# Two transformer blocks on one NeuronCore: the modulation summed on VectorE unit by unit, and the first block's values for both query tiles at once

## The chip, the cores and the metric

The kernel runs on one core of one Trainium2 chip. The metric is the device time of one execution in microseconds; where several runs are given, it is their median. The engines are named as in the profile: PE (TensorE), PEld (its weight loads), DVE (VectorE), ACT (ScalarE), POOL (GpSimd) and SP (SyncE), which issues the DMAs. Each engine takes its instructions in order; semaphores join them.

## The reference, cut to what matters

Two transformer blocks follow each other, each of two layers, on 256 tokens of width 1024, all in float32. The first block has two streams, the tokens `x` and a context `ctx` of 256 rows, and a modulation from two condition vectors: six vectors of 1024 numbers for each stream and layer, from `silu(c)` and `silu(c_ctx)` times a matrix of 1024 x 6144.

```python
for l in range(DEPTH):                       # DEPTH = 2
    mod = silu_c @ w_ada[l] + b_ada[l]       # stream x
    mod_c = silu_cc @ w_ada[l] + b_ada[l]    # stream ctx
    sh1, sc1, gt1, sh2, sc2, gt2 = jnp.split(mod[:, None, :], 6, axis=-1)
    csh1, csc1, cgt1, csh2, csc2, cgt2 = jnp.split(mod_c, 6, axis=-1)
    h = modulate(rms_norm(x, norm1_g[l]), sh1, sc1)        # h * (1 + scale) + shift
    hc = modulate(rms_norm(xc, norm1_g[l]), csh1, csc1)
    # projections of h and hc; ya: windowed attention, yb: full attention, 8 heads of 64 each
    x = x + gt1 * merge_branches(ya, yb, ga, gb, w_proj_a[l], w_proj_b[l], w_out[l])
    h2 = modulate(rms_norm(x, norm2_g[l]), sh2, sc2)
    x = x + gt2 * swiglu(h2, w_ffn_gate[l], w_ffn_up[l], w_ffn_down[l])
    if not last:
        # the same for xc, with csh2, csc2, cgt1, cgt2
```

The gates come first (`gt1` in the w_out step, `gt2` in the down step), shifts and scales in the norms. In layer 1 the context only gives keys and values, so of its modulation no more than `csh1` and `csc1` is used. The second block (three branches, no modulation) is not touched by the change.

## The kernel before

**Products.** Activations lie transposed, features on partitions, 512 columns for both streams in layer 0 and 256 in layer 1. Each weight product is made in split float32: a weight tile is loaded as 1 MB of raw numbers (`wload` L182, `rawp`, two tiles, by SP's queue), `wsplit` (L189) makes its high part on ACT (L197) and its low part on DVE (L198) into four buffers, and `product` (L201) issues three matmuls for each of eight row blocks: high times high (L204), low times high (L205), high times low (L206), into one of three PSUM banks `acc`. The splits are issued at a raised priority, so that they stand earlier in the engines' order than they are written.

**Stages of the first block, layer 0** (times in the profile): keys, values and queries of the first attention up to 83 us; the first attention woven with the projections of the second (83 to 220); the second attention woven with the first branch's gates and merge (to 336); the second branch's gates and merge (to 383); the w_out step `narrow` (L773) with the second norm (to 429); the feed-forward part in three parts of gate, up and down products (to 825); layer 1's first norm inside the last `narrow` (to 848); then layer 1.

**Modulation.** `ada` (L334) makes it in units of 512 of the 6144 columns, twelve to a layer. A unit loads four pieces of 512 KB of `w_ada` (L345; tile `araw`, two buffers), and for each piece PE makes four matmuls of 256 columns (L349) with a stationary tile `silu_c` of 32 columns of which two are used, one per stream; the four go to four groups of 32 partitions of one bank `sm` that a DVE reduce adds up later. ACT copies the unit's rows (L353), PE transposes them (L356, four at 128 columns), DVE reduces (L358), adds the bias (L361) and makes gains and halved gates (L363 to L367). The generator yields after each piece, and `tick` (L387) takes one step of the first generator in `pending`. Ticks stand in the queries, the merge, `narrow` and the feed-forward loop. Units 2, 0, 3 and 1 of layer 0 are made ahead of everything, up to 60 us. Units 4 to 11 are put in `pending` at L446; all twelve of layer 1 are put there at L805, behind the w_out step, and whatever is left is drained before the last down step of layer 0 (L890), since that step's `norm1` needs layer 1's first units.

**Attention.** `gqa_steps` (L477) goes over pairs of heads and query tiles of 128. For each it issues scores (L498, a mask matmul L501), the row maximum on DVE (L502), and then the values of the query tile before: `values_of` (L542) transposes the two heads' probabilities (L551), ACT copies them to `pts` (L553, four buffers), and PE multiplies the values (`vt`, up to four key tiles) with them into bank `y` (L557): 64 value rows, 128 query columns a matmul. After the second query tile the result is split (L560, L561).

Of the kernel before, what the change touches and what calls it, by code (L numbers as in the profile page):

```python
# [9 lines left out]
F32 = mybir.dt.float32  # L10
# [4 lines left out]
ALU = mybir.AluOpType  # L15
AX = mybir.AxisListType

P = 128
D = 1024
KD = D // P  # L20
S = 256
# [54 lines left out]
def two_blocks(ctx: ExitStack, tc: tile.TileContext, A, out: bass.AP, tap=None):  # L76
    nc = tc.nc
# [245 lines left out]
    silu_c = cp.tile([P, KD, 32], F32, name="silu_c")  # L323
# [4 lines left out]
    V.tensor_scalar(out=silu_c[:, :, 0:2], in0=th.rearrange("p (s k) -> p k s", s=2), scalar1=0.5, scalar2=None, op0=ALU.mult)  # L328
# [3 lines left out]
    hgate = [cp.tile([P, 2, 8, 2], F32, name=f"hgate_{l}") for l in range(DEPTH)]  # L332

    def ada(l, units, tiles, banks=(sm_bank, sm_bank)):  # L334

        for u in units:
# [22 lines left out]
            tl = slice(4 * u, 4 * u + 4)  # L359
            M = mod[l][:, tl, :]  # L360
            V.tensor_add(out=M, in0=d, in1=colsb[:, 48 * l + 4 * u:48 * l + 4 * u + 4].unsqueeze(2).to_broadcast([P, 4, 2]))  # L361
            kind, ks = u // 2, slice(4 * (u % 2), 4 * (u % 2) + 4)
            if kind in (1, 4):  # L363
                gain, vec = (gain1, g_norm1) if kind == 1 else (gain2, g_norm2)
                V.scalar_tensor_tensor(out=gain[l][:, ks, :], in0=M, scalar=1.0, in1=vec[l][:, ks].unsqueeze(2).to_broadcast([P, 4, 2]), op0=ALU.add, op1=ALU.mult)
            elif kind in (2, 5):
                V.tensor_scalar(out=hgate[l][:, kind // 3, ks, :], in0=M, scalar1=0.5, scalar2=None, op0=ALU.mult)  # L367
            yield

    def early():  # L370
# [7 lines left out]
        for tag, bufs in (("g", 4), ("pts", 4), ("ks", 4), ("qst", 2), ("pr", 2)):  # L378
            for _ in range(bufs // 2):
                yield [ba.tile([P, 512], F32, name="early", tag=tag, bufs=bufs) for _ in range(2)]  # L380

    def araw():
        return b1.tile([P, 1024], F32, name="araw", tag="araw", bufs=2),

    pending = []

    def tick():  # L387

        if pending:
            if next(pending[0], 0) is not None:  # L390
                pending.pop(0)
                tick()

# [52 lines left out]
    pending.append(ada(0, range(4, 12), araw))  # L446
# [30 lines left out]
    def gqa_steps(heads):  # L477
# [6 lines left out]
        for hd in heads:  # L484
# [6 lines left out]
            y = []  # L491
            for qt in range(2):
# [15 lines left out]
                before = (prs, nk, v, vt0, y, qt, dest, do)  # L508
# [33 lines left out]
    def values_of(prs, nk, v, vt0, y, qt, dest, do):  # L542

        nt = nk // P
        pts = []
        if qt == 0:
            y.append(y_bank())
        for b in range(2):
# [3 lines left out]
            pt = ba.tile([P, 4, P], F32, name="pts", tag="pts", bufs=4)  # L552
            SC.copy(out=pt[:, :nt, :], in_=bk[:, :nk].rearrange("p (k q) -> p k q", k=nt))  # L553
            pts.append(pt)
        for t in range(nt):
            for b in range(2):
                PE.matmul(y[0][64 * b:64 * b + 64, qt * P:(qt + 1) * P], lhsT=v[:, vt0 + t, 64 * b:64 * b + 64], rhs=pts[b][:, t, :],  # L557
                          start=t == 0, stop=t == nt - 1)
        if qt:
            hi, lo = dest  # L560
            SC.copy(out=hi[:, do:do + S], in_=y[0][:, :S])  # L561
            V.tensor_sub(out=lo[:, do:do + S], in0=y[0][:, :S], in1=hi[:, do:do + S].bitcast(F32))
# [10 lines left out]
    for l in range(DEPTH):  # L573
# [24 lines left out]
        def keys_values(br, k0, begun=None):  # L598
# [15 lines left out]
            vt = ba.tile([P, 4, P], F32, name="vt", tag="vt", bufs=2)  # L614
# [214 lines left out]
        for part, (f0, fn) in enumerate(((0, 8), (8, 8), (16, 6))):  # L829
# [603 lines left out]
```

## Time and profile before

| | us |
|---|---|
| runs | 1891.56, 1891.6, 1893.95 (median 1891.6) |
| profiled execution | 1890.48 |
| its span | 1888.7 |
| PE busy | 1854.9 (98%) |
| DVE busy | 1134.0 (60%) |
| ACT busy | 926.8 (49%) |
| mean granted clock of PE | 0.996 |
| modulation matmuls L349, 640 records | 53.4 |
| values matmuls L557, 640 records | 65.5 |

The page gives for the whole span each engine's busy time, then its costliest groups of instructions with the idle time of the engine just before them. A view by windows gives the same busy times for stretches of the span, and a timeline gives single groups with their start. Records of matmuls overlap: a product of 512 columns shows some 0.4 us, but the next one starts about 0.24 us later, so costs on PE are read from starts. A matmul on float32 operands, such as L557, stands as two records.

### The profile page before, as it was taken

The page shows a single profiled execution, that of the slowest core. Times are in us where ns is not written, and L with a number is a line of the kernel's source. Part 1 is how long each engine was busy: PE and PEld are TensorE (multiplying, and loading weights), DVE is VectorE, ACT ScalarE, POOL GpSimd, SP SyncE. Part 2 cuts the span into 40 slices and gives each one's busy share as a digit, 9 for nine tenths or more (in the row PEclk, how much of TensorE's full clock was granted, in tenths as well). Part 3 has the DMA queues.
Part 4 walks back from the last instruction along what each step waited for, and adds up shares of the span by engine and source line. Part 5 has one row for each costly group of instructions (what it writes and reads, how often), then busy time and mean ns, then how long its engine had stood idle before and what let it go on. Part 6 is the DMA issues. An engine that isn't in the chain of part 4 may idle for free. (4 is left out here: it accounts for less than half of the span.)

```text
span 1888.7 us, 31209 instructions
## 1 busy us (share of the span) xinstructions
PE 1854.9 (98%) x12529; PEld 1549.3 (82%) x12529; DVE 1134.0 (60%) x2518; ACT 926.8 (49%) x1759; POOL 3.4 (0%) x9
## 2 busy tenths in 40 slices
PE   7999999999999999999999999999999999999998
PEld 3666666789777777777789999988999998899997
DVE  5655433456333333359756855589876777885676
ACT  2577754334212212236775644465665456475444
POOL 0000000000000000000000000000000000000000
PEclk9999999999999999999999999999999999999999
DMA  9612334423444454353236565555444465453453
GB/s 282 178 56 68 98 101 138 145 90 101 156 145 134 133 167 144 111 181 101 57 90 171 177 202 174 159 190 162 145 133 151 144 197 179 135 157 118 151 166 124
DMA packets 266540, 269.72 MB, mean 143 GB/s; under 512 B 16162, under 2 KB 248092, under 8 KB 266396
## 3 DMA queue, kind: packets, MB, share of 16 engines
q1 hardware_dynamic: 266396, 267.73, 46.2%
q8 instruction: 99, 1.62, 0.4%
q14 instruction: 45, 0.37, 0.1%
HBM read 266.65 MB, written 1.05 MB: 142 GB/s over the span
## 5 line engine op out<-in xcount | busy, mean ns | idle before, releaser
L204 PE MATMUL acc<-hi,whi 128*128 128x256 f32 (+1 forms) x2352 | 739.5, 315 | 7.6 <-DVE ft L844 2.8
L206 PE MATMUL acc<-hi,wlo 128*128 128x256 f32 (+1 forms) x2352 | 735.6, 313 | 0.5 <-DVE wlo L198 0.5
L205 PE MATMUL acc<-lo,whi 128*128 128x256 f32 (+1 forms) x2352 | 734.6, 313 | 0.4 <-DVE lo L312 0.4
L197 ACT CAST whi<-raw 128x1024 fp32r<-128x1024 f32 (+2 forms) x422 | 401.8, 959 | 658.5 <-PE acc L205 495.5
L198 DVE TENSOR_TENSOR wlo<-raw,whi 128x1024 fp32r<-128x1024 f32 (+2 forms) x422 | 466.5, 1111 | 326.8 <-ACT whi L197 320.8
L204 PEld LDWEIGHTS acc<-hi,whi 128*128 128x128 f32 x2352 | 443.6, 189 | 51.8 <-issue 17.0
L206 PEld LDWEIGHTS acc<-hi,wlo 128*128 128x128 f32 x2352 | 444.0, 189 | 32.6 <-issue 6.2
L205 PEld LDWEIGHTS acc<-lo,whi 128*128 128x128 f32 x2352 | 444.0, 189 | 31.2 <-issue 5.1
L204 PE MATMUL acc<-uh,whi 128*128 128x256 f32 (+1 forms) x370 | 124.4, 337 | 0.8 <-ACT uh L847 0.8
L206 PE MATMUL acc<-uh,wlo 128*128 128x256 f32 (+1 forms) x370 | 123.0, 333 | 0.1
L205 PE MATMUL acc<-ul,whi 128*128 128x256 f32 (+1 forms) x370 | 122.9, 332 | 0.1
L765 DVE SCALAR_TENSOR_TENSOR x<-acc,hgate,x 128x256 f32<-128x256 f32 x64 | 30.8, 482 | 103.7 <-PE acc L206 103.5
L502 DVE TENSOR_REDUCE nm<-sc 128x1 f32<-128x512 f32 (+1 forms) x96 | 55.6, 597 | 57.6 <-PE sc L498 44.8
L204 PEld LDWEIGHTS acc<-uh,whi 128*128 128x128 f32 x370 | 69.6, 188 | 15.9 <-issue 9.1
L206 PEld LDWEIGHTS acc<-uh,wlo 128*128 128x128 f32 x370 | 69.6, 189 | 8.5 <-issue 1.6
L205 PEld LDWEIGHTS acc<-ul,whi 128*128 128x128 f32 x370 | 69.7, 188 | 7.9 <-issue 1.2
L557 PE MATMUL y<-pts,vt 128*64 128x128 f32 x640 | 65.5, 284 | 0.0
L553 ACT COPY pts<-pt 128x512 f32<-128x512 f32 (+1 forms) x96 | 49.2, 513 | 32.6 <-PE pt L551 31.4
L557 PEld LDWEIGHTS y<-pts,vt 128*64 128x64 f32 x640 | 42.6, 136 | 22.6 <-issue 13.8
L846 DVE TENSOR_TENSOR ft<-ft,acc 128x256 f32<-128x256 f32 (+1 forms) x42 | 22.9, 546 | 59.6 <-PE acc L206 58.7
L498 PE MATMUL sc<-ks,qst 128*128 128x512 f32 (+1 forms) x192 | 56.2, 388 | 0.0
L349 PE MATMUL sm<-araw,silu_c 128*32 128x256 f32 x640 | 53.4, 391 | 2.4 <-DMA araw<-in_w_ada_dram 2.2
(463 smaller groups left out, 2431.0 us busy)
## 6 DMA issues: line engine op xcount, KB each, us to landing
raw<-in_w_in_dram SPq DMA_DIRECT2D x90, 1024.0 KB
araw<-in_w_ada_dram SPq DMA_DIRECT2D x80, 512.0 KB
raw<-in_w_ffn_gate_dram SPq DMA_DIRECT2D x22, 1024.0 KB
raw<-in_w_ffn_up_dram SPq DMA_DIRECT2D x22, 1024.0 KB
raw<-in_w_out_dram SPq DMA_DIRECT2D x16, 1024.0 KB
raw<-in_w_ffn_down_dram SPq DMA_DIRECT2D x16, 1024.0 KB
raw<-in_w_branch_dram SPq DMA_DIRECT2D x12, 1024.0 KB
raw<-in_w_in_dram SPq DMA_DIRECT2D x18, 512.0 KB
```

The lines of the kernel that those rows point to most:

```text
L197: SC.copy(out=h, in_=src)
L198: V.tensor_sub(out=l_, in0=src, in1=h.bitcast(F32))
L204: PE.matmul(o, lhsT=w[0][:, k, :], rhs=xs[0][k][:, sl], start=first, stop=False)
L205: PE.matmul(o, lhsT=w[0][:, k, :], rhs=xs[1][k][:, sl], start=False, stop=False)
L206: PE.matmul(o, lhsT=w[1][:, k, :], rhs=xs[0][k][:, sl], start=False, stop=last)
L349: PE.matmul(b[32 * q:32 * q + 32, 256 * c:256 * c + 256], lhsT=silu_c[:, 4 * z + q, :], rhs=r[q], start=z == 0, stop=z == 1, skip_group_ch ...
L498: PE.matmul(sp, lhsT=qst[:, b, qt * P:(qt + 1) * P], rhs=ks[b][z][:, ko:ko + nk], start=z == 0, stop=z == 1 and not band)
L502: V.tensor_reduce(out=nm[:, b:b + 1], in_=sp, axis=AX.X, op=ALU.max, negate=True)
L553: SC.copy(out=pt[:, :nt, :], in_=bk[:, :nk].rearrange("p (k q) -> p k q", k=nt))
L557: PE.matmul(y[0][64 * b:64 * b + 64, qt * P:(qt + 1) * P], lhsT=v[:, vt0 + t, 64 * b:64 * b + 64], rhs=pts[b][:, t, :], start=t == 0, stop ...
L765: V.scalar_tensor_tensor(out=streams[s][j], in0=b, scalar=hgate[l][:, which, j, s:s + 1], in1=streams[s][j], op0=ALU.mult, op1=ALU.add)
L846: V.tensor_mul(out=t, in0=t, in1=bu)
```

## The change

**Modulation.** Units 4 to 11 of layer 0 and all of layer 1 are made by a new generator `ada_sums`. A unit's rows come in eight pieces of 128 rows by 512 columns (256 KB; `araw` has three buffers of 512 columns now). For each piece and stream DVE multiplies it with that row block's column of `silu` and adds it to the running sum: the first piece by a plain multiplication, the others by `scalar_tensor_tensor`. Stream 0's sum stands in the first piece's own `araw` tile, stream 1's in a new tile `asum`. Then PE transposes the sum (four at 128 columns) and DVE reduces it over 128 partitions' worth of columns, for each stream by itself; `finish_mod` has the rest as before. Units 4 to 11 of layer 1 are made for stream `x` alone (ns = 1). The units made early keep the old way through PE.

**Where it is asked for.** `need_mod(l, u)` takes ticks until unit u is there. It stands before the w_out step (unit 9), before each down step (unit 11) and before the last down step of layer 0 (unit 3 of layer 1), in place of the two drains; what is left of layer 1's units runs on into layer 1.

**Values.** `values_of` issues the transposes and copies for each query tile as before, into `pts` tiles that hold both query tiles (two buffers of twice the size for four), and the values matmuls only with the second query tile: 64 value rows, 256 query columns each, half as many.

```diff
-    silu_c = cp.tile([P, KD, 32], F32, name="silu_c")
+    silu = cp.tile([P, KD, 2], F32, name="silu")
+    silu_c = ba.tile([P, 512], F32, name="silu_c", tag="vt", bufs=2)[:, :32 * KD].rearrange("p (k c) -> p k c", k=KD)
...
-    V.tensor_scalar(out=silu_c[:, :, 0:2], in0=th.rearrange("p (s k) -> p k s", s=2), scalar1=0.5, scalar2=None, op0=ALU.mult)
+    V.tensor_scalar(out=silu, in0=th.rearrange("p (s k) -> p k s", s=2), scalar1=0.5, scalar2=None, op0=ALU.mult)
+    V.tensor_copy(out=silu_c[:, :, 0:2], in_=silu)
...
-    def araw():
-        return b1.tile([P, 1024], F32, name="araw", tag="araw", bufs=2),
...
+    def ada_sums(l, units):
+
+
+        for u in units:
+            ns = 2 if l == 0 or u < 4 else 1
+            d = small.tile([P, 4, 2], F32, name="modsum", tag="modsum")
+            for k in range(KD):
+                r = b1.tile([P, 512], F32, name="araw", tag="araw", bufs=3)
+                nc.sync.dma_start(out=r, in_=A["w_ada"][l][k * P:(k + 1) * P, 512 * u:512 * u + 512])
+                if k == 0:
+
+                    sums_ = [r, b1.tile([P, 512], F32, name="asum", tag="asum", bufs=1)][:ns]
+                for s_ in reversed(range(ns)):
+                    c = silu[:, k, s_:s_ + 1]
+                    if k == 0:
+                        V.tensor_scalar(out=sums_[s_], in0=r, scalar1=c, scalar2=None, op0=ALU.mult)
+                    else:
+                        V.scalar_tensor_tensor(out=sums_[s_], in0=r, scalar=c, in1=sums_[s_], op0=ALU.mult, op1=ALU.add)
+                if k % 2 and k < KD - 1:
+                    yield
+            for s_ in range(ns):
+                o = sm_bank()
+                for q in range(4):
+                    PE.transpose(o[:, q * P:(q + 1) * P], sums_[s_][:, q * P:(q + 1) * P], ident)
+                V.tensor_reduce(out=d[:, :, s_:s_ + 1], in_=o.rearrange("p (t r) -> p t r", t=4), axis=AX.X, op=ALU.add)
+                if s_ < ns - 1:
+                    yield
+            finish_mod(l, u, d, ns)
+            summed.add((l, u))
+            yield
...
+    def need_mod(l, u):
+
+        while (l, u) not in summed:
+            tick()
...
-    pending.append(ada(0, range(4, 12), araw))
+    pending.append(ada_sums(0, range(4, 12)))
...
-    def values_of(prs, nk, v, vt0, y, qt, dest, do):
+    def values_of(prs, nk, v, vt0, pts, qt, dest, do):
 
         nt = nk // P
-        pts = []
         if qt == 0:
-            y.append(y_bank())
+            pts += [ba.tile([P, 4, 2, P], F32, name="pts", tag="pts", bufs=2) for _ in range(2)]
         for b in range(2):
             bk = pt_bank()
             for t in range(nt):
                 PE.transpose(bk[:, t * P:(t + 1) * P], prs[b][:, t * P:(t + 1) * P], ident)
-            pt = ba.tile([P, 4, P], F32, name="pts", tag="pts", bufs=4)
-            SC.copy(out=pt[:, :nt, :], in_=bk[:, :nk].rearrange("p (k q) -> p k q", k=nt))
-            pts.append(pt)
-        for t in range(nt):
-            for b in range(2):
-                PE.matmul(y[0][64 * b:64 * b + 64, qt * P:(qt + 1) * P], lhsT=v[:, vt0 + t, 64 * b:64 * b + 64], rhs=pts[b][:, t, :],
-                          start=t == 0, stop=t == nt - 1)
+            SC.copy(out=pts[b][:, :nt, qt, :], in_=bk[:, :nk].rearrange("p (k q) -> p k q", k=nt))
         if qt:
+            y = y_bank()[:, :S]
+            for t in range(nt):
+                for b in range(2):
+                    PE.matmul(y[64 * b:64 * b + 64, :], lhsT=v[:, vt0 + t, 64 * b:64 * b + 64], rhs=pts[b][:, t].rearrange("p q c -> p (q c)"),
+                              start=t == 0, stop=t == nt - 1)
...
+        need_mod(l, 9)
         narrow(A["w_out"][l], 0, KD, ms, 0, 1, norm2 if both else None)
         if both:
-            pending.append(ada(1, range(12), araw))
-            while len(pending) > 1:
-                tick()
+            pending.append(ada_sums(1, range(12)))
...
             final = part == 2
+            need_mod(l, 11)
             if final and both:
-                while pending:
-                    tick()
+                need_mod(1, 3)
```

**The order on PE**, at one query tile of the second attention in layer 0, between products of the merge. Before (`pt`: transposed probabilities, `y`: values, `sc`: scores of the next tile):

```order
L551 MATMUL pt<-consts,pr 128x128 x4
L206 MATMUL acc<-hi,wlo 128x512
L204 MATMUL acc<-hi,whi 128x512
L205 MATMUL acc<-lo,whi 128x512
L206 MATMUL acc<-hi,wlo 128x512
L551 MATMUL pt<-consts,pr 128x128 x4
L557 MATMUL y<-pts,vt 64x128
L498 MATMUL sc<-ks,qst 128x256 x2
L204 MATMUL acc<-hi,whi 128x512
L557 MATMUL y<-pts,vt 64x128 x7
L498 MATMUL sc<-ks,qst 128x256 x2
```

The same place after the change (L595, L601 and L543 are the same lines as L551, L557 and L498):

```order
L595 MATMUL pt<-consts,pr 128x128 x4
L204 MATMUL acc<-hi,whi 128x512
L205 MATMUL acc<-lo,whi 128x512
L206 MATMUL acc<-hi,wlo 128x512
L204 MATMUL acc<-hi,whi 128x512
L595 MATMUL pt<-consts,pr 128x128 x4
L601 MATMUL y<-pts,vt 64x256
L543 MATMUL sc<-ks,qst 128x256 x2
L205 MATMUL acc<-lo,whi 128x512
L601 MATMUL y<-pts,vt 64x256 x7
L543 MATMUL sc<-ks,qst 128x256 x2
```

The place of the values is the same, one matmul ahead of the scores and seven behind a product; each is 256 columns wide, and at the other query tile none stands.

**The order on DVE**, at the end of the second branch's merge in layer 0 (`msum` and `macc` empty a product's bank, `wlo` and `lo` are low parts of weights and of activations). Before:

```order
L739 SCALAR_TENSOR_TENSOR msum<-g,acc 128x512
L743 TENSOR_TENSOR macc<-msum,macc 128x512
L198 TENSOR_TENSOR wlo<-raw,whi 128x1024
L222 TENSOR_TENSOR lo<-macc,hi 128x512
L739 SCALAR_TENSOR_TENSOR msum<-g,acc 128x512
L198 TENSOR_TENSOR wlo<-raw,whi 128x1024
L743 TENSOR_TENSOR macc<-msum,macc 128x512
L739 SCALAR_TENSOR_TENSOR msum<-g,acc 128x512
L743 TENSOR_TENSOR macc<-msum,macc 128x512
```

After (L782 and L786 are the same as L739 and L743; L413 is the new sum):

```order
L782 SCALAR_TENSOR_TENSOR msum<-g,acc 128x512
L413 SCALAR_TENSOR_TENSOR asum<-araw,silu,asum 128x512
L786 TENSOR_TENSOR macc<-msum,macc 128x512
L413 SCALAR_TENSOR_TENSOR araw<-araw,silu 128x512
L782 SCALAR_TENSOR_TENSOR msum<-g,acc 128x512
L198 TENSOR_TENSOR wlo<-raw,whi 128x1024
L786 TENSOR_TENSOR macc<-msum,macc 128x512
L413 SCALAR_TENSOR_TENSOR asum<-araw,silu,asum 128x512
L413 SCALAR_TENSOR_TENSOR araw<-araw,silu 128x512
L782 SCALAR_TENSOR_TENSOR msum<-g,acc 128x512
L413 SCALAR_TENSOR_TENSOR asum<-araw,silu,asum 128x512
L786 TENSOR_TENSOR macc<-msum,macc 128x512
```

Sums of both streams now stand between the operations that empty the products' banks and the splits of the weights.

**The order of the DMAs on SP**, at the beginning of the feed-forward part of layer 0. Before:

```order
L183 DMA raw<-in_w_ffn_gate_dram 128x8x256
L345 DMA araw<-in_w_ada_dram 128x4x256 x2
L183 DMA raw<-in_w_ffn_up_dram 128x8x256
L345 DMA araw<-in_w_ada_dram 128x4x256 x3
L183 DMA raw<-in_w_ffn_gate_dram 128x8x256
```

After:

```order
L183 DMA raw<-in_w_ffn_up_dram 128x8x256
L404 DMA araw<-in_w_ada_dram 128x512 x5
L183 DMA raw<-in_w_ffn_gate_dram 128x8x256
L404 DMA araw<-in_w_ada_dram 128x512
L183 DMA raw<-in_w_ffn_up_dram 128x8x256
L404 DMA araw<-in_w_ada_dram 128x512 x4
```

Pieces of the modulation's weights, half as large, stand between the 1 MB loads in the same manner, up to five in a row.

## Rows read from the trace of the kernel before

**Rows 1.** The page's first part: busy us, share of the span, instructions by engine.

```profile
PE 1854.9 (98%) x12529; PEld 1549.3 (82%) x12529; DVE 1134.0 (60%) x2518; ACT 926.8 (49%) x1759; POOL 3.4 (0%) x9
```

**Rows 2.** Windows: us, then PE, PEld, DVE, ACT, POOL busy; PEclk, DMA share, GB/s.

```profile
60.00:83.00 23.00, 23.00 (x118) 16.52 (x117) 18.22 (x39) 13.35 (x20) 0.00 (x0) 1.00 0.44 118
83.00:336.00 253.00, 252.35 (x1510) 169.75 (x1508) 113.33 (x320) 164.20 (x382) 0.00 (x0) 1.00 0.33 98
336.00:429.00 93.00, 92.88 (x499) 76.49 (x499) 51.79 (x94) 31.42 (x49) 0.00 (x0) 1.00 0.38 113
429.00:825.00 396.00, 393.66 (x2019) 297.69 (x2019) 153.36 (x252) 102.99 (x147) 0.00 (x0) 1.00 0.46 144
825.00:906.00 81.00, 79.77 (x529) 64.18 (x528) 68.79 (x190) 47.30 (x97) 0.00 (x0) 1.00 0.35 104
906.00:970.00 64.00, 63.69 (x503) 52.46 (x503) 43.76 (x114) 51.44 (x111) 0.00 (x0) 1.00 0.31 83
```

**Rows 3.** Timeline of PE around one modulation group: start us, us, instructions.

```profile
511.18 0.40 PE L205 MATMUL acc<-lo,whi 128*128 128x512 f32 x1
511.42 0.40 PE L206 MATMUL acc<-hi,wlo 128*128 128x512 f32 x1
511.74 0.64 PE L349 MATMUL sm<-araw,silu_c 128*32 128x256 f32 x8
512.31 0.50 PE L204 MATMUL acc<-hi,whi 128*128 128x512 f32 x1
512.65 0.40 PE L205 MATMUL acc<-lo,whi 128*128 128x512 f32 x1
```

**Rows 4.** Page part 5, the modulation matmuls: busy, mean ns; idle before, releaser.

```profile
L349 PE MATMUL sm<-araw,silu_c 128*32 128x256 f32 x640 | 53.4, 391 | 2.4 <-DMA araw<-in_w_ada_dram 2.2
```

**Rows 5.** Timeline of PE around one unit's four transposes.

```profile
500.95 0.39 PE L205 MATMUL acc<-lo,whi 128*128 128x512 f32 x1
501.19 0.60 PE L356 MATMUL sm<-consts,modrow 128*128 128x128 f32 x4
501.54 0.48 PE L206 MATMUL acc<-hi,wlo 128*128 128x512 f32 x1
501.86 0.39 PE L204 MATMUL acc<-hi,whi 128*128 128x512 f32 x1
```

**Rows 6.** Timeline of PE around values: fourteen records, then two behind transposed probabilities.

```profile
225.31 0.39 PE L205 MATMUL acc<-yl,whi 128*128 128x512 f32 x1
225.63 1.09 PE L557 MATMUL y<-pts,vt 128*64 128x128 f32 x14
226.64 0.50 PE L206 MATMUL acc<-yh,wlo 128*128 128x512 f32 x1
226.98 0.39 PE L204 MATMUL acc<-yh,whi 128*128 128x512 f32 x1
...
230.04 0.40 PE L204 MATMUL acc<-yh,whi 128*128 128x512 f32 x1
230.28 0.60 PE L551 MATMUL pt<-consts,pr 128*128 128x128 f32 x4
230.80 0.43 PE L557 MATMUL y<-pts,vt 128*64 128x128 f32 x2
231.17 0.50 PE L205 MATMUL acc<-yl,whi 128*128 128x512 f32 x1
231.50 0.40 PE L206 MATMUL acc<-yh,wlo 128*128 128x512 f32 x1
```

**Rows 7.** DVE by line and form: busy us, mean ns; idle before.

```profile
L1146 DVE SCALAR_TENSOR_TENSOR ca<-mu,cols_conv,ca 128x256 f32<-128x256 f32 x48 | 23.0, 479 | 0.5
L844 DVE SCALAR_TENSOR_TENSOR ft<-ft,acc 128x512 f32<-128x512 f32 x20 | 13.6, 680 | 0.0
L539 DVE TENSOR_SCALAR pr<-pr,sm 128x512 f32<-128x512 f32 x16 | 7.7, 484 | 0.7
L1150 DVE SCALAR_TENSOR_TENSOR mq<-zt,ca 128x256 f32<-128x256 f32 x16 | 6.7, 419 | 0.5
```

More of the change, by code (lines that the diff above doesn't have):

```diff
@@ L332, in two_blocks @@
     hgate = [cp.tile([P, 2, 8, 2], F32, name=f"hgate_{l}") for l in range(DEPTH)]
+    GP.memset(mod[1], 0.0)
     def ada(l, units, tiles, banks=(sm_bank, sm_bank)):
@@ L358, in ada @@
             V.tensor_reduce(out=d, in_=o.rearrange("p (t q r) -> p t r q", t=4, q=4)[:, :, 0:2, :], axis=AX.X, op=ALU.add)
[L359 to L367, printed above, removed]
+            finish_mod(l, u, d)
             yield
@@ L377, in early @@
             yield wp.tile([P, 1024], F32, name="early", tag="whi" if n % 2 else "wlo"),
-        for tag, bufs in (("g", 4), ("pts", 4), ("ks", 4), ("qst", 2), ("pr", 2)):
+        for _ in range(2):
+            t = ba.tile([P, 4, 2, P], F32, name="early", tag="pts", bufs=2)
+            yield t.rearrange("p a b c -> p (a b c)"),
+        for tag, bufs in (("g", 4), ("ks", 4), ("qst", 2), ("pr", 2)):
             for _ in range(bufs // 2):
                 yield [ba.tile([P, 512], F32, name="early", tag=tag, bufs=bufs) for _ in range(2)]
-    def araw():
-        return b1.tile([P, 1024], F32, name="araw", tag="araw", bufs=2),
@@ L385, in two_blocks, with finish_mod @@
     pending = []
+    summed = set()
+    def finish_mod(l, u, d, ns=2):
+        tl = slice(4 * u, 4 * u + 4)
+        M = mod[l][:, tl, :ns]
+        V.tensor_add(out=M, in0=d[:, :, :ns], in1=colsb[:, 48 * l + 4 * u:48 * l + 4 * u + 4].unsqueeze(2).to_broadcast([P, 4, ns]))
+        kind, ks = u // 2, slice(4 * (u % 2), 4 * (u % 2) + 4)
+        if kind in (1, 4):
+            gain, vec = (gain1, g_norm1) if kind == 1 else (gain2, g_norm2)
+            V.scalar_tensor_tensor(out=gain[l][:, ks, :ns], in0=M, scalar=1.0, in1=vec[l][:, ks].unsqueeze(2).to_broadcast([P, 4, ns]), op0=ALU.add, op1=ALU.mult)
+        elif kind in (2, 5):
+            V.tensor_scalar(out=hgate[l][:, kind // 3, ks, :ns], in0=M, scalar1=0.5, scalar2=None, op0=ALU.mult)
@@ L490, in gqa_steps @@
                 V.tensor_sub(out=qst[oth, b, :], in0=q[own, qo:qo + S], in1=qst[own, b, :].bitcast(F32))
-            y = []
+            pts = []
             for qt in range(2):
@@ L507, in gqa_steps @@
                 prs = softmax_pair(sps, nk, nm, i, qt, sinks, rq)
-                before = (prs, nk, v, vt0, y, qt, dest, do)
+                before = (prs, nk, v, vt0, pts, qt, dest, do)
                 yield
@@ L551, in values_of @@
                 PE.transpose(bk[:, t * P:(t + 1) * P], prs[b][:, t * P:(t + 1) * P], ident)
[L552 to L559 removed]
+            SC.copy(out=pts[b][:, :nt, qt, :], in_=bk[:, :nk].rearrange("p (k q) -> p k q", k=nt))
+        if qt:
+            y = y_bank()[:, :S]
[3 more added lines that the diff above has]
+                              start=t == 0, stop=t == nt - 1)
             hi, lo = dest
[L561 to L562 removed]
+            SC.copy(out=hi[:, do:do + S], in_=y)
+            V.tensor_sub(out=lo[:, do:do + S], in0=y, in1=hi[:, do:do + S].bitcast(F32))
     gfw = cp.tile([P, KD], F32, name="gfw")
@@ L613, in keys_values @@
             product(vraw, w, hs, KD, al, 4 if begun else 0)
-            vt = ba.tile([P, 4, P], F32, name="vt", tag="vt", bufs=2)
+            vt = ba.tile([P, 512], F32, name="vt", tag="vt", bufs=2).rearrange("p (t c) -> p t c", t=4)
             vf = wide("vf")
```

## The prediction

> **What bounds the kernel now.** I read the busy times first: TensorE (PE) works 1854.9 us of 1888.7, VectorE (DVE) 1134.0, ScalarE (ACT) 926.8 [rows 1]. Then the busy times by stage, in the stretch that the change touches [rows 2]: PE is busy 98.5% to 100% of every stage at a granted clock of 1.00, DMA engines 31% to 46%, DVE between 39% (the feed-forward part, 429 to 825 us) and 85% (825 to 906 us). So whatever leaves PE shortens the program one for one, as long as DVE, ACT and the DMA queue keep up; and where DVE stood at 85%, PE lost 1.2 of 81 us, its worst stage. The third view is PE's record of instructions around the groups that the change removes or merges [rows 3]: what such a group costs is read from the starts of the products around it, since the durations overlap.
>
> All sums go against the profiled execution's own 1890.5 us; the median of the runs, 1891.6, is 1.1 above it, and that is added at the end.
>
> **What leaves PE: the modulation products.** Two products in a row start 0.24 us apart [rows 3]. With a group of eight modulation records between them, two products further on start at 512.65 instead of 511.42 + 0.47, so the group costs 1.23 - 0.47 = 0.76, say 0.77 us. There are 640 records, 80 groups [rows 4]; most stand alone like this one. 80 x 0.77 = **-61.6 us**. Where two stand together they share the ramp, so a little less is possible: at the mean record of 53.4 us in all, the lower end is -53. I take 61.6, since by the order over two thirds of the groups stand alone.
>
> **What comes to PE: transposes.** The sums on DVE end in 4 transposes per unit and stream, 32 groups, in place of one per unit, 20 groups: 12 more. A group of four costs (501.86 - 500.95) - 0.47 = 0.44 us [rows 5]: **+5.3 us**.
>
> **The values of the first block.** The order shows 320 matmuls of 128 columns before, in 48 groups of one, 16 of three and 32 of seven; after it, 160 of 256 columns in 24, 8 and 16 such groups. Each stands as two records in the trace. A group of seven (14 records) costs (226.98 - 225.31) - 0.47 = 1.20; a group of one (2 records), behind four transposes, (231.50 - 230.04) - 0.47 - 0.44 = 0.55 [rows 6]. So 0.055 us for a record of 128 columns and 0.44 for opening and closing a group. Before: 48 x 0.55 + 16 x 0.77 + 32 x 1.21 = 77.4. After, with columns at the same price (0.11 for a record of 256): 24 x 0.66 + 8 x 1.10 + 16 x 1.98 = 56.3. **-21.1 us**, which is just the 48 groups that go. The columns are as many as before; this term hangs on the group's price alone, and its low end is zero.
>
> Sum on PE: -61.6 + 5.3 - 21.1 = -77.4, so 1813.1 us if nothing else moves.
>
> **What comes to DVE, and whether it hides.** 256 operations of 512 columns: 32 multiplications by a column, 0.484 us [rows 7], and 224 multiply-adds. The trace has no multiply-add of this form and width; the nearest rows are the one of 512 columns without a column scalar, 0.680, and the pair of 256 columns with and without, 0.479 and 0.419 [rows 7]. So 0.68 + 0.06 = 0.74, and 0.71 as the mean of the 256. Ends: 0.48 (as the multiplication) and 1.26 (rival 3). 32 reduces of 512 elements are priced as another 512-wide pass, 0.68. In all +204 us, DVE to about 1338. By the order these fall on the stages of [rows 2] so (sums, reduces):
>
> 60 to 83: 14, 0; DVE 18.2 + 10 = 28, PE 23.0 - 3 x 0.77 = 20.7.
> 83 to 336: 82, 10; DVE 113.3 + 65 = 178, PE 253 - 19 - 13 + 2 = 223 (80%).
> 336 to 429: 48, 6; DVE 51.8 + 38 = 90, PE 93 - 3 + 1 = 91 (99%).
> 429 to 825: 90, 11; DVE 153.4 + 71 = 225, PE 396 - 35 + 2 = 363 (62%).
> 825 to 970: 22, 5; DVE 112.6 + 19 = 132, PE 145 - 7 = 138 (95%).
>
> The unit order explains the shape: the units that the w_out products, the down products and the second layer's first norm need must be done by then, and after those points nothing is forced. The new work stands in DVE's queue ahead of what PE waits for: the low weight halves (split four ahead), the merge sums that give a PSUM bank back, the head's query split before the scores. Where DVE has 60% to 80% I charge what the 85% stage lost before, 1.5% of 223: 3 to 4 us, taken as 4. The two stages at 95% and 99% have no slack over their length; some 5% there, 5 and 7. In the first stretch DVE has 7 us more work than PE; ten sums stand before the first split of the queries, and part is caught up later: 5. **+21 us**, with ends 0 (all hidden by split-ahead buffers) and 53 (every stage at 95% or above 15% longer, 14 for the others and the whole 7 in the first). The waits of PE's modulation products for their weights go, 2.2 us [rows 4]. ACT loses the 20 copies of the modulation rows, and the DMA bytes are the same in 160 pieces of 256 KB for 80 of 512; at a DMA share of 0.46 or less and with PE's queue no longer waiting for them, I cost both at nothing. What is late next, where a stall goes, is DVE.
>
> 1890.5 - 77.4 + 21 - 2.2 + 1.1 = 1833; **forecast 1832 us**, own range 1816 to 1850.
>
> **The rivals.**
> 1. Forecast as above: 0.58.
> 2. No new waits: sums run in DVE's gaps everywhere. For it: DVE's mean share stays below 75%. Against: the stages at 95% and 99%. 1813 - 2 + 1 = 1812: 0.15.
> 3. The multiply-add of two SBUF tiles runs at half rate. From [rows 7], 256 columns at 0.419 and 512 at 0.680 give 1.02 ns a column and 0.16 fixed; at twice the slope 0.16 + 1.04 + 0.06 = 1.26 us. Then DVE has 35 for 21, 222 for 223, 115 for 91, 272 for 363 and 143 for 138 us: waits of some 12 + 10 + 24 + 2 + 9 = 57, so 1813 + 57 - 2 + 1 = 1869. Against it: the row of 0.419 has both tiles in SBUF and lies on the same line as the row of 0.680 with a PSUM operand. 0.13, for that and for any other way in which DVE bounds the dense stages. The Trainium skill says it as a rule (Vector Engine (DVE) Microarchitecture Reference, section 7, Points that are easy to get wrong): the scalar-tensor-tensor form with two non-bf16 sources in SBUF halves its throughput. The row named above speaks against it at 256 columns; no row here shows it at 512 with a column scalar.
> 4. The grouping saves nothing, because the price of a values group goes with its columns, or the groups' gaps come back as waits for the two query tiles' copies (pts has two tiles of both query tiles now, and the PSUM bank for the values is opened only at the second one). Then the 21.1 is missing: 1853. For it: the columns are the same. Against: 0.55 for two records and 1.20 for fourteen [rows 6] leave 0.44 that no column pays. 0.09. The Trainium skill (TensorE: Matmul & The Clock Gate, section Back-to-back issue gap) gives a warm gap of N/2.4 + 2.5 ns, by which half as many matmuls of twice the width would save an estimated 0.8 us in all; the rows show the group's price, which this formula has not.
> 5. Slower: the head of DVE's in-order queue waits for a weight piece. The pieces are loaded by SyncE's in-order queue between the 1 MB loads of the products, and these wait until DVE has made the low halves of earlier weights; only two pieces can be under way, as the third tile is the sum. A sum that stands at DVE's head without its piece then holds the low halves, PE, and the next loads. It decides from 77 / 160 = 0.48 us of PE's time per piece; a whole landing at 144 GB/s [rows 2] is 1.8 us, so 43 unhidden pieces do. With half of them, 80 x 1.8 = 144: 1813 + 144 = 1957. Against it: PE waited for this same stream, equally two pieces deep, for 2.2 us in 80 groups [rows 4]. 0.05.
>
> **How the numbers follow.** The range goes from the no-wait case to above the missing grouping, 1810 to 1860; left out are rivals 3 and 5, about 0.17. 0.2% (3.8 us) is about what a measurement of this kernel can tell from no change. Cases 1 to 4 are faster by more; rival 5 is slower, but for a narrow strip: faster 0.94, same 0.02, slower 0.04.
>
> **What would show it.** Right: no modulation matmuls in this stretch; PE shorter by about 77 us in busy time; values 48 groups with records of about twice the length; multiply-adds of 0.74 us; PE idle grown by some 20 us, most of it in 336 to 429 and around the second layer's first norm, with DVE as the releaser. Multiply-adds near 1.26 us and PE waits for the low halves near 55 us would show rival 3; values of the same total as before, rival 4; DVE idle before the sums with their weight pieces as the releaser, and PE idle behind it, rival 5. The forecast is wrong if the group prices that PE pays come from the modulation's small tiles in a way that a plain stream of products doesn't give back, or if the added waits exceed 40 us.

## The result

The changed kernel takes 1839.4 us (four runs, 1835.3 to 1841.2) against 1892.4 for the kernel before (four runs beside it, 1891.6 to 1894.0). The ratio is 0.9716, with a 95% interval of 0.9698 to 0.9734: 53 us, or 2.8%. The forecast was 1832, its own range 1816 to 1850, the whole range 1810 to 1860. The direction and the range held; three terms of the sum were off and in part cancelled, which the experiments take apart.

The page of the changed kernel, part 1 and then part 5 (columns as in [rows 1] and [rows 4]):

```profile
PE 1791.5 (97%) x11617; PEld 1529.5 (83%) x11617; DVE 1301.4 (71%) x2787; ACT 916.9 (50%) x1739; POOL 3.6 (0%) x10
...
L413 DVE SCALAR_TENSOR_TENSOR araw<-araw,silu 128x512 f32<-128x512 f32 x140 | 104.6, 747 | 26.7 <-DMA araw<-in_w_ada_dram 26.6
...
L413 DVE SCALAR_TENSOR_TENSOR asum<-araw,silu,asum 128x512 f32<-128x512 f32 x84 | 62.7, 747 | 8.6 <-DMA araw<-in_w_ada_dram 8.4
...
L601 PE MATMUL y<-pts,vt 128*64 128x256 f32 x320 | 56.8, 401 | 0.0
```

PE's busy time fell by 63 us and its idle time grew from 33.8 (1888.7 - 1854.9) to 47.8 us. A multiply-add takes 747 ns; the prediction had estimated 740 from [rows 7]. No modulation matmul is left in this stretch, and the values have half as many records, 401 ns instead of 284 each.

DVE's busy time grew by 167 us, to 1301.4, and not by the 204 of the prediction. Its new records do add up to 205 us (104.6 and 62.7 above, the multiplications 9.7 and 5.7, the reduces 21.9, of which 3.8 were there before), but on DVE too a record overlaps the next one: in a row, multiply-adds of 0.75 us start 0.66 us apart.

```profile
83.33 0.75 DVE L413 SCALAR_TENSOR_TENSOR araw<-araw,silu 128x512 f32<-128x512 f32 x1
83.99 0.75 DVE L413 SCALAR_TENSOR_TENSOR asum<-araw,silu,asum 128x512 f32<-128x512 f32 x1
84.65 0.75 DVE L413 SCALAR_TENSOR_TENSOR araw<-araw,silu 128x512 f32<-128x512 f32 x1
```

The stages of the changed kernel by windows (columns as in [rows 2]):

```profile
85.30:208.10 122.80, 120.44 (x610) 78.50 (x609) 95.24 (x261) 100.18 (x247) 0.00 (x0) 1.00 0.31 91
208.10:308.20 100.10, 100.10 (x502) 74.70 (x501) 72.64 (x140) 59.80 (x129) 0.00 (x0) 1.00 0.43 119
308.20:400.00 91.80, 91.05 (x475) 75.99 (x473) 82.64 (x147) 29.97 (x46) 0.00 (x0) 1.00 0.52 160
400.00:782.00 382.00, 380.08 (x1815) 313.11 (x1813) 234.55 (x389) 106.48 (x150) 0.00 (x0) 1.00 0.46 144
782.00:930.00 148.00, 142.29 (x910) 110.40 (x909) 116.87 (x303) 102.49 (x216) 0.00 (x0) 0.98 0.36 103
```

Stages that begin and end at the same events in every kernel can be set side by side. In the table each stage ends with the event named, read from the first or last start of that DVE operation; lengths in us:

| stage ends at | before | changed | changed again | values only | sums only | thin sums | two steps |
|---|---|---|---|---|---|---|---|
| first score maximum | 83.5 | 85.3 | 85.0 | 82.4 | 87.6 | 81.1 | 85.3 |
| first merge sum, branch 0 | 136.9 | 122.8 | 122.7 | 131.9 | 125.2 | 123.5 | 122.9 |
| first merge sum, branch 1 | 115.7 | 100.1 | 100.0 | 111.7 | 105.5 | 100.3 | 100.1 |
| first residual of w_out | 51.1 | 54.1 | 53.9 | 51.1 | 54.6 | 50.6 | 54.9 |
| last residual of layer 0 | 460.0 | 419.7 | 419.2 | 460.4 | 420.0 | 421.0 | 420.0 |
| last score maximum, layer 1 | 141.5 | 148.0 | 146.6 | 137.6 | 145.1 | 139.7 | 137.7 |
| last residual of layer 1 | 264.8 | 273.1 | 270.5 | 265.2 | 271.5 | 269.6 | 270.0 |
| end (second block) | 635.2 | 636.2 | 642.1 | 639.6 | 634.8 | 638.6 | 636.4 |

Layer 0 gained 65 us (847.2 to 782.0 at its end); layer 1 gave 15 back (6.5 + 8.3). The last row is code that no kernel here changes; it lies between 635 and 642 in these profiles, so a difference of a few us in one profile's last row says nothing. Between the two traces of the changed kernel the rows of layer 0 differ by 0.5 us at most, those of layer 1 by 1.4 and 2.6.

### The profile page after: what moved, and what is told of

It is laid out like the page before. It is cut to its first block, busy times and chain, and to the rows that moved or that the text cites. A ratio compares the mean times of both kernels' runs of the same rounds, so it can differ in the third digit from the quotient of the medians.

```text
span 1839.3 us, 29868 instructions
## 1 busy us (share of the span) xinstructions
PE 1791.5 (97%) x11617; PEld 1529.5 (83%) x11617; DVE 1301.4 (71%) x2787; ACT 916.9 (50%) x1739; POOL 3.6 (0%) x10
## 4 chain that ended last, share of the span: by engine, by line
PE 80%; DVE 9%; DMA 7%; ACT 3%; issue 1%; SPq 0%; ACTq 0%; DVEq 0%
PE acc L206 21%; PE acc L204 21%; PE acc L205 21%; DVE wlo L198 3%; PE y L601 3%; PE sc L543 2%; PE pt L595 2%; DMA raw<-in_w_ffn_up_dram 2%; DMA araw<-in_w_ada_dram 2%; ACT whi L197 1%; DMA raw<-in_w_ffn_down_dram 1%; PE acc L975 1%; PE acc L977 1%; PE acc L976 1%; PE y L1214 1%
## 5 line engine op out<-in xcount | busy, mean ns | idle before, releaser
L413 DVE SCALAR_TENSOR_TENSOR araw<-araw,silu 128x512 f32<-128x512 f32 x140 | 104.6, 747 | 26.7 <-DMA araw<-in_w_ada_dram 26.6
L413 DVE SCALAR_TENSOR_TENSOR asum<-araw,silu,asum 128x512 f32<-128x512 f32 x84 | 62.7, 747 | 8.6 <-DMA araw<-in_w_ada_dram 8.4
L543 PE MATMUL sc<-ks,qst 128*128 128x512 f32 (+1 forms) x192 | 56.5, 390 | 2.1 <-ACT pr L572 1.5
L601 PE MATMUL y<-pts,vt 128*64 128x256 f32 x320 | 56.8, 401 | 0.0
L595 PE MATMUL pt<-consts,pr 128*128 128x128 f32 x320 | 53.0, 280 | 3.6 <-ACT pts L596 2.0
```

Source lines behind the costliest of these rows:

```text
L413: V.scalar_tensor_tensor(out=sums_[s_], in0=r, scalar=c, in1=sums_[s_], op0=ALU.mult, op1=ALU.add)
L543: PE.matmul(sp, lhsT=qst[:, b, qt * P:(qt + 1) * P], rhs=ks[b][z][:, ko:ko + nk], start=z == 0, stop=z == 1 and not band)
L595: PE.transpose(bk[:, t * P:(t + 1) * P], prs[b][:, t * P:(t + 1) * P], ident)
L601: PE.matmul(y[64 * b:64 * b + 64, :], lhsT=v[:, vt0 + t, 64 * b:64 * b + 64], rhs=pts[b][:, t].rearrange("p q c -> p (q c)"), start=t == 0 ...
```

## The experiments

**The changed kernel once more.** No edit.

> The changed kernel itself once more, for its spread and a second trace. The profiled run of it lost 6.5 us between the end of layer 0 and the last scores of layer 1 (142 us before, 148 after, PE dry at 887 us and its clock at 0.50 behind that) and 8 more up to the second block. Theory A (the new order of sums, weight pieces and values in layer 1 makes PE run dry there): the second trace shows the same gap at the same place, 148 us again. Theory B (chance of one execution: a late load, the clock falls once PE is idle): the stretch is nearer to 142 and the time lower, 1835 us, as in the one run of 1835.34 at a clock of 0.996.

Measured 1841.4 us (1834.9 to 1842.4), ratio 0.9716. The stretch of layer 1 is long again, 146.6 us, with the same stretch without a product on PE (from 885.8 us, 11.5 us long): theory A. It belongs to the kernel and not to one execution.

**The values alone.** On the kernel before: `pts` with both query tiles, and

```diff
-        for t in range(nt):
-            for b in range(2):
-                PE.matmul(y[0][64 * b:64 * b + 64, qt * P:(qt + 1) * P], lhsT=v[:, vt0 + t, 64 * b:64 * b + 64], rhs=pts[b][:, t, :],
...
+            for t in range(nt):
+                for b in range(2):
+                    PE.matmul(y[64 * b:64 * b + 64, :], lhsT=v[:, vt0 + t, 64 * b:64 * b + 64], rhs=pts[b][:, t].rearrange("p q c -> p (q c)"),
...
```

> The kernel before with the values grouped for both query tiles and nothing else. The sum of the prediction: 48 groups fewer at 0.44 us, 21 us, so about 1871 us, ratio 0.989. If the price of values goes with its columns, or the gaps come back as waits: within 4 us of the kernel before, ratio 0.998 to 1.002. If grouping makes PE run dry in layer 1's attention, the stretch from the end of layer 0 to the last scores stays at 141 us or grows, instead of losing 5 to 8 of its 141.5.

Measured 1882.7 us beside 1892.9, ratio 0.9942 (0.9927 to 0.9958): 8 to 14 us, not 21 and not nothing. The three stages with values lose 5.0, 4.0 and 3.9 us, 13 in all. PE's timeline of this kernel shows the price of a group of wider records:

```profile
223.11 0.60 PE L553 MATMUL pt<-consts,pr 128*128 128x128 f32 x4
223.64 0.65 PE L559 MATMUL y<-pts,vt 128*64 128x256 f32 x2
224.22 0.50 PE L205 MATMUL acc<-yl,whi 128*128 128x512 f32 x1
224.56 0.40 PE L206 MATMUL acc<-yh,wlo 128*128 128x512 f32 x1
224.88 1.94 PE L559 MATMUL y<-pts,vt 128*64 128x256 f32 x14
226.75 0.50 PE L204 MATMUL acc<-yh,whi 128*128 128x512 f32 x1
227.09 0.40 PE L205 MATMUL acc<-yl,whi 128*128 128x512 f32 x1
```

Fourteen records cost (227.09 - 224.56) - 0.47 = 2.06 us. The pair, from the transposes' start to the second product, takes 1.45 for 1.22 in [rows 6], so 0.78 for 0.55. The record's price is as assumed, (2.06 - 0.78) / 12 = 0.107; but opening and closing a group costs 0.78 - 0.21 = 0.57 us, not 0.44. With 24 groups of 0.78, 8 of 1.21 and 16 of 2.06 the values cost 61.4 for 77.4 before: 16 us, not 21. Why a group of wider records costs more to open and close, no run shows.

**The sums alone.** On the changed kernel the values as before.

```diff
-    def values_of(prs, nk, v, vt0, pts, qt, dest, do):
+    def values_of(prs, nk, v, vt0, y, qt, dest, do):
...
+        for t in range(nt):
+            for b in range(2):
+                PE.matmul(y[0][64 * b:64 * b + 64, qt * P:(qt + 1) * P], lhsT=v[:, vt0 + t, 64 * b:64 * b + 64], rhs=pts[b][:, t, :],
...
         if qt:
-            y = y_bank()[:, :S]
...
```

> The changed kernel with the values as before, one query tile at a time. If the two parts add up with the prediction's 21 us for the values, this takes 1839 + 21 = 1860 us, ratio 0.983 to the kernel before; the prediction's own sum for this part (61.6 out, 5.3 in, 21 of waits, 2 of old waits gone) says 1855. If grouping gave nothing, it is at 1839. If the grouped values are what lets PE run dry in layer 1, this kernel keeps its 142 us there and loses less than the 21.

Measured 1842.3 us, ratio 0.9730 (0.9714 to 0.9745): 51 us from the sums by themselves, where the prediction's part said 37. So on top of the sums, grouping brought 1 us here (1841.4 on the same chip; both times are uncertain by some 3 us). The table shows a part of where it went. By the end of layer 0 grouping has won 11 us (782.0 for 792.9), most of it in the two stages up to the second branch's merge (2.4 + 5.4) and at the start (2.3). Layer 1's attention is longer by 1.5 to 3, where grouping alone had saved 4. The rest can't be placed: it lies in the spread between executions.

**Thin sums.**

```diff
-                        V.scalar_tensor_tensor(out=sums_[s_], in0=r, scalar=c, in1=sums_[s_], op0=ALU.mult, op1=ALU.add)
+                        V.scalar_tensor_tensor(out=sums_[s_][:, :32], in0=r[:, :32], scalar=c, in1=sums_[s_][:, :32], op0=ALU.mult, op1=ALU.add)
```

> The changed kernel with its multiply-adds on 32 of the 512 columns (the other columns hold only the first row block's product): same loads, same count of DVE instructions, same transposes, but each sum short; DVE loses about 224 x 0.6 = 134 us. If the waits that the prediction charged (21 us) are DVE's load, this gains 15 to 20 us on the changed kernel: about 1820. If the sums are hidden and what is lost is lost to loads and the order of issue, it gains less than 4 us: 1835 to 1839.

Measured 1824.8 us, 16.6 below the changed kernel on the same chip. A multiply-add still takes 0.25 us, so 106 of DVE's 167 us are gone (busy 1195.5 us), not the 134 that were estimated. The instructions of each kernel are put in order anew, and this order differs from the changed kernel's in some hundred places on PE. So the 16.6 us are what this part of DVE's load costs by waits and by order together; no run parts the two. They stand where the table says: 4.2 us before the first score maximum (seven products fewer stand ahead of the first scores here, which is 1.7 us of it at 0.24 each), 3.5 before the first residual of w_out, and 8.3 behind layer 0; the merge and the feed-forward part pay nothing. The window of that last stretch, for [rows 2] and the fifth row above:

```profile
776.50:916.20 139.70, 137.33 (x898) 108.47 (x897) 111.20 (x300) 100.97 (x213) 0.00 (x0) 1.00 0.38 109
```

**The last sums drained before layer 1.** In the changed kernel 13 of the 256 sums run on into layer 1.

```diff
-                need_mod(1, 3)
+                need_mod(1, 11)
```

> The changed kernel with all sums of layer 1 asked for before the last down step of layer 0, so that layer 1 holds none of the 13 sums that ran on into it. Theory: these 13 sums (10 us of DVE) stand in the stretch from the end of layer 0 to layer 1's last scores, where DVE also has the norm and the softmax; the kernel with thin sums took 139.7 us for it against 148 and 146.6. Then this one takes 139 to 141 there, and gives back 0 to 4 us in the feed-forward part (372.9): 1833 to 1836 in all. Rival: the stretch is long because of the grouped values (PE had no products left at 887 us): it stays at 146 to 148, and the time at 1839 to 1842.

Measured 1855.2 us, ratio 0.9803 (0.9782 to 0.9825): 14 us worse than the changed kernel, which neither theory expected. The sums did leave layer 1's attention, but as one burst at the end of layer 0: PE's transposes of the sums stand in PE's order between its last products, and the last of them behind these, ahead of layer 1's norm. PE's waits between 60 and 960 us (waiting line, releaser, us in total, times, longest) and the windows there:

```profile
PE sm L419 <- DVE araw L413: 17.0, 4, 12.5
```

```profile
780.00:800.00 20.00, 7.53 (x41) 7.35 (x42) 10.93 (x17) 2.98 (x4) 0.00 (x0) 0.67 0.62 206
800.00:810.00 10.00, 5.93 (x26) 5.07 (x25) 6.69 (x28) 2.51 (x6) 0.00 (x0) 0.50 0.01 2
```

One transpose waits 12.5 us, up to 799.6, for a sum whose pieces come one by one between 1 MB loads. The granted clock is 0.67 over the window of this wait and 0.50 in the next. The two theories on layer 1's attention are not told apart by this kernel; the next one does.

**Two steps in the feed-forward part.** The same, and

```diff
                         inner(u, lat)
                         tick()
+                        tick()
```

> As the one before, but with two steps of the sums instead of one behind each pair of gate and up products, so that they are spread over the feed-forward part of layer 0, where DVE has 63% to do, and are done before its last down step. Theory: the stretch behind layer 0 falls to 139 to 141 us, the feed-forward part stays within 1 us of 372.9; 1832 in all, 8 us better than the changed kernel. Rival (grouped values): 146 to 148 there, 1840 in all.

Measured 1829.1 us, ratio 0.9665 (0.9639 to 0.9690), and once more on another chip 1830.5, ratio 0.9659 (0.9645 to 0.9672): 10 us better than the changed kernel. The stretch behind layer 0 falls from 148.0 to 137.7 us:

```profile
783.20:920.90 137.70, 135.88 (x887) 106.78 (x885) 106.97 (x278) 101.41 (x213) 0.00 (x0) 1.00 0.30 86
```

> The kernel with two steps of the sums behind each pair of gate and up products once more, beside the three that are built on it, on one chip. Expected as in its first run, about 1829 us, the stretch behind layer 0 at 138 us.

So without the 13 sums in layer 1 the 10 us are back. How they cost so much is seen in PE's timeline of the changed kernel (start us, us; in brackets idle before and releaser):

```profile
886.96 0.28 PE L205 MATMUL acc<-yl,whi 128*128 128x256 f32 x1
887.08 0.28 PE L206 MATMUL acc<-yh,wlo 128*128 128x256 f32 x1
888.08 1.50 PE L543 MATMUL sc<-ks,qst 128*128 128x512 f32 x4 [0.73 <-ACT pr L572]
890.85 0.81 PE L595 MATMUL pt<-consts,pr 128*128 128x128 f32 x4 [1.27 <-DVE nm L566]
892.33 1.12 PE L595 MATMUL pt<-consts,pr 128*128 128x128 f32 x4 [0.68 <-ACT pts L596]
893.38 1.12 PE L601 MATMUL y<-pts,vt 128*64 128x256 f32 x2
894.42 1.22 PE L543 MATMUL sc<-ks,qst 128*128 128x512 f32 x2
895.58 3.11 PE L601 MATMUL y<-pts,vt 128*64 128x256 f32 x14
```

```profile
888.00:892.00 4.00, 2.28 (x8) 1.04 (x8) 3.19 (x8) 3.62 (x7) 0.00 (x0) 0.89 0.00 0
892.00:896.00 4.00, 3.67 (x10) 1.81 (x12) 1.35 (x2) 2.40 (x6) 0.00 (x0) 0.50 0.67 129
```

From 887.4 to 899.9 us no product stands in PE's order: scores, softmax, transposes and values of two query tiles follow each other bare, and each waits for the one before on ACT or DVE. PE idles 2.0 us in two waits, then its granted clock is at 0.50, the 1.2 GHz level (1.00 up to 891.1 us, 0.50 from 891.2 to 897.9), and the seven values matmuls take 3.11 us instead of 1.94. DVE is not full there, with 3.19 of 4 and 1.35 of 4 us. The order of the kernel with two steps has products between the same instructions: its longest stretch without one is 5.7 us.

The sums do not make this gap alone. The kernel with the sums alone has the same 13 sums in this stretch, no place of more than 4.6 us without a product, and a granted clock of 1.00:

```profile
792.90:938.00 145.10, 142.81 (x1027) 116.04 (x1026) 116.79 (x303) 102.43 (x216) 0.00 (x0) 1.00 0.36 105
```

It takes 145.1 us, for 141.4 in the two-step kernel with single values below. So the sums by themselves cost some 4 us there, and the other 5 to 7 come with sums and grouped values together; the rival had a part in it. That the two pushed the products out of this place when the order was planned is argued from the orders, not shown by itself.

**Another queue for the pieces.**

```diff
-                nc.sync.dma_start(out=r, in_=A["w_ada"]
+                nc.gpsimd.dma_start(out=r, in_=A["w_ada"]
```

> The changed kernel with the 256 KB weight pieces issued by GpSimd's queue instead of SyncE's, where they stand between the 1 MB loads and DVE waited 35 us in all for pieces. If PE loses time because sums at DVE's head wait for pieces that stand behind held 1 MB loads (rival 5 of the prediction, small), this gains 4 us or more: below 1836. If DVE's waits for pieces are covered by the four split weights ahead of PE: 1838 to 1842, no difference.

Measured 1866.4 us, ratio 0.9856 (0.9825 to 0.9886): 25 us worse, against both expectations. DVE's waits between 60 and 900 us:

```profile
DVE araw L413 <- DMA araw<-in_w_ada_dram: 83.8, 42, 6.6
...
DVE asum L413 <- DMA araw<-in_w_ada_dram: 27.4, 23, 3.4
```

DVE stands 111 us at sums whose piece isn't there, for 35 in the changed kernel. The edit also moved sums to earlier places in DVE's order (the first one stands at 9.4 us among the first norm's statistics, for 71.2 us in the changed kernel), so it doesn't separate the queue from the order. What it shows is that these waits of DVE and the 25 us come together.

**Sums made twice.**

```diff
-                        V.scalar_tensor_tensor(out=sums_[s_], in0=r, scalar=c, in1=sums_[s_], op0=ALU.mult, op1=ALU.add)
+                        for _ in range(2):
+                            V.scalar_tensor_tensor(out=sums_[s_], in0=r, scalar=c, in1=sums_[s_], op0=ALU.mult, op1=ALU.add)
```

> The changed kernel with each of the 224 multiply-adds made twice in a row: 167 us more on DVE, 1.5 us for a piece and stream instead of 0.75, nearly the half rate of rival 3, with every wait for loads as it is. Rival 3's sum said 57 us of waits in place of 21, so about 36 us over the changed kernel: 1876. If the cost goes on as between the thin and the whole sums (15 us for 134 us of DVE, 0.11 per us), it is 19 us more: 1858. If the buffers ahead take it, under 8: 1845.

Measured 1889.6 us, ratio 0.9975 (0.9963 to 0.9987): 48 us over the changed kernel, more than any of the three, and nearly all of the change's gain. The price is not linear: 0.16 us per us of DVE's busy time from thin to whole sums (16.6 for 106), 0.33 from whole to double (48 for 146, busy 1446.9), the changed orders included in both. The stage that bore most is the end of the merge, 40.7 us for 25.0 from the first split of its result (DVE's first `lo<-macc,hi`) to the first residual; its window and PE's waits between 300 and 420 us:

```profile
368.80:409.50 40.70, 28.32 (x114) 21.37 (x113) 39.12 (x63) 10.13 (x15) 0.00 (x0) 0.79 0.38 119
```

```profile
PE acc L204 <- DVE msum L783: 12.3, 3, 6.5
PE acc L206 <- DVE wlo L198: 6.1, 2, 3.2
```

DVE is busy 96% of it, and PE waits for the operation that gives a bank back and for the low weight halves, as named in the prediction; the clock falls to 0.79 on top.

**Two steps, the values one query tile at a time.** The two-step kernel with the values part undone, as in the sums alone.

> The same with the values one query tile at a time, as in the kernel before. Over the changed kernel's schedule grouping was worth only about 2 us, over the kernel before 10 to 13. Theory: in layer 1 the sums hid what grouping saves, since PE waited there for DVE and not for its own work; with the sums gone from layer 1, grouping is worth its 11 us of layer 0 and its 4 of layer 1, so this kernel takes 1840 to 1843. Rival: grouping costs waits of its own wherever sums are near; then it is worth 2 to 5 us here too, 1831 to 1834.

Measured 1843.2 us beside 1830.5: grouping is worth 12.7 us here, as the first theory said. It is worth 10 to 13 on this kernel and on the kernel before. In the changed kernel it costs 1.5 to 3 us in layer 1's attention instead of saving 4, by the gap above.

**Fewer sums in the first queries, and then in the merge.** Both are built on the kernel with two steps, the second on the first.

```diff
-                if i >= len(begun):
-                    tick()
-                for _ in range(len(begun) if i == 3 else 0):
+                if br:
                     tick()
```

> Two steps in the feed-forward part, and no step of the sums in the first attention's queries, so that none of the first ten sums stands on DVE ahead of the first query split. With thin sums the stretch to the first score maximum was 4.2 us shorter (81.1 for 85.3). Theory: this gains 3 to 4 us there and gives at most 1 back later: 1825 to 1827. Rival: the sums that move fall into stages that DVE fills as well, and the 4 us come back in the merge or the w_out step: 1829.

```diff
-                    tick()
+                    if br == 0:
+                        tick()
...
+            need_mod(l, 9)
...
-        need_mod(l, 9)
+        need_mod(l, 5)
```

> The one before with fewer sums in the second branch's merge, which DVE fills to 85% and more: no step in its second halves, units 6 to 9 asked for only by the second norm. With thin sums the stretch from the first split to the first residual was 3 us shorter (22.0 for 25.0), the next one 2 us longer. Theory: 1 to 3 us gained there and none lost in the feed-forward part, where DVE has room: 1823 to 1826. Rival: the second norm then waits for units 6 to 9, whose pieces and transposes are asked for in one burst, as in the drain before layer 1, which cost 17 us of PE waiting for sums: 1835 or more.

Measured 1828.2 and 1829.4 us beside 1830.5, ratios 0.9642 (0.9625 to 0.9660) and 0.9653 (0.9639 to 0.9668) beside 0.9659: no gain that these runs can tell, and the second meets neither of its expectations. In the traces the first moves the first score maximum from 85.6 to 79.1 us and gives 3.2 us back in the second attention (103.3 for 100.1); the second shortens the way from the first split to the first residual from 26.0 to 20.9 and lengthens the next two stages by 5. At layer 1's last score maximum the two stand 2.7 and 6.4 us ahead; what follows is unchanged code that differs by as much from profile to profile.

## Why the prediction was right, and where it was off

- **What bounds.** Right: PE was full, and what left it shortened the program while DVE kept up.
- **Modulation out, transposes in** (-56.3 and -2.2 predicted). Right. The feed-forward part, from the first output of the second norm (427.4 us before, 400.0 after) to the last residual of layer 0, lost 48 groups of modulation matmuls and got one group of transposes more. By the prediction's prices that is 48 x 0.77 - 0.44 = 36.5 us; it fell from 419.8 to 382.0, by 37.8. At the mean of the records [rows 4], 0.67 a group, it would have been 32, so the price read from starts [rows 3] holds.
- **Values** (-21.1 predicted). The term that was mis-sized. The price for opening and closing a group was taken from records of 128 columns and kept for 256, where it is 0.57 and not 0.44. By that the term is -16, and the runs give -10.2 alone and -12.7 on the two-step kernel. The 3 to 6 us between are not accounted for. In the changed kernel itself grouping brought only 1 us, since the gap in layer 1 comes with it. Rival 4 is wrong in its mechanism, as columns alone don't make the price, but the missing gain that it named did come about in the changed kernel, by another way.
- **New waits** (+21 predicted, of them 5, 4, 5 and 7). Thin sums give 16.6 for 106 of DVE's 167 us, changed order included; the price of the rest was not measured. The stages show 4, 0, 1.5 (3.5, of which the next stage gives 2 back) and 8. The sums alone give less: of the 58.5 us that the modulation was to bring, 50.6 came, so 8 were lost. What lies between is for the most part the gap in layer 1, which the prediction had not named. So the 21 was too much for the waits that it meant, though in place at both ends; the first merge and the dense w_out step cost less than charged. One reason is in the rows: the prediction added whole records to a busy time in which records overlap, so from the second branch's merge to the second norm DVE came to 90% (82.64 of 91.80 us) where it had forecast 99%. PE's idle time grew by 14 us instead of some 20, and by 0.6 us only from 336 to 429 us [rows 2], where most of it was expected (0.75 us in the third window above). The mechanism named for the last place was not the one at work: DVE's queue was not what PE waited for, but an order that left softmax without products beside it, and the clock behind that. The feed-forward part bore all its sums for nothing, and the two-step kernel uses that.
- **The sum.** Its terms give 1833, put down as 1832, 7 us too low. With the grouping at 12.7 and the waits at 16.6, thin sums leave 55.4 us for the modulation (68.1 - 12.7): values 8.4 short, modulation 3.1 short, waits 4.4 better. The three close by the way they are taken, and the gap that needs sums and grouping stands under the waits. That too large a saving and too large a charge met is luck in part. The upper end of the waits, 53, is 55 by its own terms; nothing rests on it.
- **Rivals.** No new waits: wrong by the 16.6. Half rate: wrong at 747 ns for its 1.26 us. The sums made twice put 168 us of records on DVE and cost 48, 0.29 per us; rival 3 had charged 36 for 116 us more, 0.31 per us. So its price for a DVE with little slack was about right, though it left out the clock's part, which showed at the end of the merge. Rival 5 didn't occur in the changed kernel, where DVE waited 35 us for pieces and PE did not; its mechanism was met in the burst before layer 1 (12.5 us for one transpose), and DVE's part of it with the other queue (111 us of waits for pieces).
- **Open.** From layer 1's last score maximum to its last residual the kernels with sums take 266.9 to 273.1 us, the two without 264.8 and 265.2, though no sum stands there. In the kernel before, the changed one in both traces, and those with values alone, sums alone and thin sums, ACT waits 47 to 56 us for the 1 MB loads in the feed-forward part of this stage. No run tells why.

## What to carry to other kernels

Price a merged or removed group of small matmuls from the starts of its neighbours, and take its fixed part from a group as wide as the new one. Price the work that an engine receives from starts as well, since its records overlap too. The work moved here to an engine at 60% was free in the merge and the feed-forward part, where that engine then stood at 61 to 78%, and cost time in other stages, so spread such work by stages and not by need: one more step per iteration of a long, slack loop was worth 10 us here, and asking for the same work in one burst cost 14. After a move, look for stretches of the bounding engine's order that have lost their filler work; two changes can do together what neither does alone.

## What the runs showed of the hardware

A float32 multiply-add of two SBUF tiles with a column scalar takes 747 ns at 512 columns, where [rows 7] has 680 with a PSUM operand and no column scalar: no halving, so the Trainium skill's rule (Vector Engine (DVE) Microarchitecture Reference, section 7, Points that are easy to get wrong) doesn't hold for this form here. In a row, the next one starts 0.66 us later.

In the changed kernel PE's clock fell though PE was never idle for over 1.3 us at a time: it was busy 1.72 of the 3.1 us from 888.0 to 891.1 us at a granted clock of 1.00, and then stood at 0.50 up to 897.9 us; in the second trace the lower level lasted 3.3 us. The waits cost more than their own length: at 0.50, fourteen values records took 3.11 us instead of 1.94.
